# A two-layer hybrid decoder block: gate by tanh, gate projected ahead of the values, shared masks, one scaling product, two gain rows moved

## The chip, the cores and the metric

The kernel runs on one core of a Trainium2 chip. A core has five engines that run at the same time, each with its own instruction queue: TensorE (PE, matrix products; its weight loads are shown as PEld), VectorE (DVE), ScalarE (ACT), GpSimd (POOL) and SyncE (SP, which here only issues DMAs). The metric is the device time of one execution in microseconds, the median over several runs.

## The reference, cut to what matters

Two layers over 512 tokens of width 1024, in fp32. Each layer computes, from `h = x * (1 + sc1) + sh1`, one input projection whose columns feed three mixers:

- a gated MLP over chunks of 128 tokens (gMLP): GELU, a norm over 64 columns, a causal product over tokens;
- retention, 4 heads of 64: queries and keys are rotated, scores within a chunk are weighted by a decay mask, a state runs from chunk to chunk; the output is normed over each head and multiplied by `silu(g)`, where g is its own projection (`rg` in the kernel; q, k and v are `rq`, `rk`, `rv`);
- sparse attention, 8 heads on 2 key groups, with three branches, each weighted by a sigmoid gate per head and token: over compressed keys, over selected blocks, over a window. Here 512 tokens hold exactly the 8 blocks of 64 that are selected, and the window spans 512 tokens, so both of these are full causal attention, each with its own keys and values.

Then an output projection, `x = layer_norm(ALPHA * x + g1 * y)`, a gated feed-forward part with a causal convolution of width 3, and a second `layer_norm`. The shifts, scales and gates (adaLN) are products of the condition vector with `w_ada`.

## The kernel before, in words

Tokens are cut into 4 blocks of 128 (index t, i or c). Every fp32 product is made of three products of rounded parts (`mm3`, L445 to L447; `tm`, L538 to L540): each weight tile of 512 KB is loaded by SyncE's queue, rounded by ScalarE (L125) and its rest formed by VectorE or, for the retention and output weights, by GpSimd (L127). `Weights` holds the tiles as one list of jobs in the order of use, loaded up to three ahead.

The order on each engine is not quite that of the program text. A planner simulates the kernel and lets each engine take the earliest instruction of the program that is ready in the simulation; `tc.keep_in_program_order` pins an instruction behind the one traced before it on its engine.

One layer runs like this. (1) Projections of query and compressed keys; the gMLP's two halves U and Vv (`za0`, `za1`, GELU at L735); the compression's small products. (2) `cmp_scores` (L691), the values with the gates' columns (`vg`), then the norm of Vv (`norm64`, L464 to L475), the softmax over the compressed scores (transposes L702, softmax L707 to L718), the key projections `k`, the transposes of the softmax (L727) and the gMLP product (L808). (3) The attention's units: a unit is a head pair hp, a branch b (selected or window) and a block i. `scores` (L953 to L968) makes two products per head, adds the causal mask as a product of a bf16 identity with the mask (L955), takes the maximum, exponentiates on ScalarE (L964) and scales by reciprocal sum and gate (L968). Block 0 of both branches goes through `scores0` at once (L979 to L991). `transposes` (L999, L1000) and `pv_mm` (L1007, L1014) follow; scores are made two units ahead. Between the units `filler` runs one step of `retention` at a time: the four projections (`tm_all`, 8 steps each), then the chunks (L890 to L929), then the norm and the gate's product (L935). In layer 0 the steps also take adaLN products (L324). (4) Output projection, norms, feed-forward part.

X holds the residual. The last norm of layer 0 leaves its rows without gain; `last_gains(t)` multiplies X[t] by `lgr` and adds `lbr` in layer 1 (`gains`, L1143 and L1144, each 128x1024), rows 0 and 1 behind `za0`, rows 2 and 3 behind `cmp_scores`. `lgr`, `lbr`, U, Vv, the rotated queries and keys, the values `vb` and the gate `gb` share five buffers of the tag `m4`.

Of the kernel before, what the change touches and what calls it, by code (L numbers as in the profile page):

```python
# [13 lines left out]
AF = mybir.ActivationFunctionType  # L14
OP = mybir.AluOpType
AX = mybir.AxisListType

P = 128
S = 512
D = 1024  # L20
NT = S // P
# [12 lines left out]
C_ZA, C_QB, C_KB, C_VB, C_GB = 0, 512, 768, 1024, 1280  # L34
# [114 lines left out]
def tile_trunk(ctx, tc, I, tab, out, layers=L):  # L149
    nc = tc.nc  # L150
    V, A, G, T = nc.vector, nc.scalar, nc.gpsimd, nc.tensor
# [80 lines left out]
    for l in range(layers):  # L232
        if l == 0:
            for k in range(KD):
                rowk = I["w_in"][0][k * P:(k + 1) * P, :]
                jobs.append((("s", k), 768, [(lambda t: t[:, :768], rowk[:, C_QC:C_QC + 768])]))
        else:
            job_cols(("kc", l), l, [(C_KCM, P)])
            job_cols(("vc", l), l, [(C_VCM, P)])
            for r in range(4):  # L240
                job_cols(("q", l, r), l, [(C_QC + HD * (r + 4 * a), HD) for a in range(2)])
        job_tm(("za0", l), l, [(C_ZA, 256)])
        job_tm(("za1", l), l, [(C_ZA + 256, 256)])
        for k0, k1 in VGK:
            job_cols(("vg", l, k0), l, [(C_VSL, 128), (C_VWN, 152)], k0, k1)
        for b, c0 in enumerate((C_KSL, C_KWN)):
            job_cols(("k", l, b), l, [(c0, P)])
        aj = [j for bank in (1, 2) for j in ada_jobs(l, bank)] if l == 0 else []
        for n in range(32):
            if n % 8 in (0, 2):  # L250
                nm, c0 = (("rq", C_QB), ("rk", C_KB), ("rv", C_VB), ("rg", C_GB))[n // 8]
                h = n % 8 // 2
                job_cols((nm, l, h), l, [(c0, 256)], 4 * h, 4 * h + 4)
            if n in ADA_AT and aj:
                j = aj.pop(0)
                if j:
                    jobs.append(j)
        jobs.extend(j for j in aj if j)
        for cc, h in WO_ORDER:
            job_rows(("wo", l, cc, h), I["w_out"][l], 512 * h, 256, cc * 256, 4)  # L260
        wu = I["w_up"][l]
        for ct in range(NFF):
            for b in range(2):
                job_rows(("up", l, ct, b), wu, 0, P, b * DFF + ct * P, KD)
        for kk in range(NFF):
            job_rows(("dn", l, kk), I["w_down"][l], kk * P, D, 0, 1)
# [245 lines left out]
    for l in range(layers):  # L512
# [252 lines left out]
        next(za1)  # L765
        cmp_scores(kc)
        run(za1)
        if l:
            for t in range(2, NT):
                last_gains(t)  # L770


        VS = h4("vs", F32).rearrange("p b (t n) -> p b t n", t=NT)
        gates = pool.tile([P, NT, 24], F32, tag="gates", name="gates", bufs=1)
# [64 lines left out]
        def retention():  # L839
# [24 lines left out]
            for j, nm in enumerate(("rq", "rk")):  # L864
                def put(tp, pz, j=j):
                    for s in range(2):
                        rotate(pz[:, s * 256:(s + 1) * 256], R[j][:, 2 * tp + s, :], 2 * tp + s,
                               zx[:, 4 * j:4 * j + 4])
                yield from tm_all((nm, l), put)
            vb, gb = m4("vb"), m4("gb")  # L870
            yield from tm_all(("rv", l), lambda tp, pz: A.copy(vb[:, tp * 512:(tp + 1) * 512], pz))

            def put_g(tp, pz):
                d = gb[:, tp * 512:(tp + 1) * 512]
                A.activation(d, pz, AF.Exp, scale=-1.0)
                V.tensor_scalar(d, d, 1.0, None, op0=OP.add)
                V.reciprocal(d, d)
                V.tensor_tensor(d, d, pz, op=OP.mult)
            yield from tm_all(("rg", l), put_g)
            yield "projected"  # L880
            o = R[0].rearrange("p c n -> p (c n)")
            st = pool.tile([P, 4, HD], F32, tag="state", name="state", bufs=1)
# [49 lines left out]
            for hf in range(2):  # L932
                hs = slice(hf * 512, (hf + 1) * 512)
                norm64(o[:, hs], bl[:, 0, :], bl[:, 1, :], V)
                V.tensor_tensor(gb[:, hs], gb[:, hs], o[:, hs], op=OP.mult)  # L935
                yield
            RB["yb"] = gb

# [3 lines left out]
        def scores(hp, b, i):  # L942

            g = hp // 2
            n = P * (i + 1)
            if i == 1:
                bank = ps()
                o = [bank[:, e * 256:e * 256 + n] for e in range(2)]
            else:
                o = [ps()[:, :n] for e in range(2)]  # L950
            for e in range(2):
                qs = Q[g][:, 2 * (hp % 2) + e, i * P:(i + 1) * P]
                T.matmul(o[e], qs, KH[:, 2 * b + g, :n], start=True, stop=False)  # L953
                T.matmul(o[e], qs, KL[:, 2 * b + g, :n], start=False, stop=False)  # L954
                T.matmul(o[e][:, i * P:n], identb, cmaskb, start=False, stop=True)  # L955
            sm = pool.tile([P, 4, 2], F32, tag="sm", name="sm", bufs=4)
            if i == 1:
                V.reduce_max(sm[:, 0, :], bank.rearrange("p (e n) -> p e n", e=2)[:, :, :n], axis=AX.X, negate=True)
            else:
                for e in range(2):  # L960
                    V.reduce_max(sm[:, 0, e:e + 1], o[e], axis=AX.X, negate=True)  # L961
            pp = [pt(), pt()]
            for e in range(2):
                A.activation(pp[e][:, :n], o[e], AF.Exp, bias=sm[:, 0, e:e + 1], accum_out=sm[:, 1, e:e + 1])  # L964
            V.reciprocal(sm[:, 2, :], sm[:, 1, :])
            for e in range(2):
                c = 3 * (2 * hp + e) + 1 + b
                V.tensor_scalar(pp[e][:, :n], pp[e][:, :n], sm[:, 2, e:e + 1], gates[:, i, c:c + 1],  # L968
                                op0=OP.mult, op1=OP.mult)
            return pp  # L970

        def scores0(hp):
# [3 lines left out]
            for e in range(2):  # L976
                o = bank[:, e * 256:(e + 1) * 256].rearrange("p (b n) -> p b n", b=2)
                qs = Q[g][:, 2 * (hp % 2) + e, :P]
                T.matmul(o, qs, KH[:, g::2, :P], start=True, stop=False)  # L979
                T.matmul(o, qs, KL[:, g::2, :P], start=False, stop=False)  # L980
                T.matmul(o, identb, cmaskb[:, None, :].to_broadcast([P, 2, P]), start=False, stop=True)
            sm = pool.tile([P, 4, 2], F32, tag="sm", name="sm", bufs=4).rearrange("p (a c) b -> p a (c b)", a=2)
            b4 = bank.rearrange("p (j n) -> p j n", j=4)
            V.reduce_max(sm[:, 0, :], b4, axis=AX.X, negate=True)
# [1 line left out]
            for j in range(4):  # L986
                A.activation(pp[:, j, :], b4[:, j, :], AF.Exp, bias=sm[:, 0, j:j + 1], accum_out=sm[:, 1, j:j + 1])
            V.reciprocal(sm[:, 1, :], sm[:, 1, :])
            for j in range(4):
                c = 3 * (2 * hp + j // 2) + 1 + j % 2  # L990
                V.tensor_scalar(pp[:, j, :], pp[:, j, :], sm[:, 1, j:j + 1], gates[:, 0, c:c + 1],  # L991
                                op0=OP.mult, op1=OP.mult)
            return [[pp[:, 2 * e + b, :] for e in range(2)] for b in range(2)]

        def transposes(i, pp, PT):
# [354 lines left out]
        if l + 1 < layers:  # L1350
# [3 lines left out]
            def last_gains(t, gains=gains, lgr=lgr, lbr=lbr):  # L1354
                gains(t, lgr, lbr)
# [28 lines left out]
```

## Time and profile before

| | |
|---|---|
| runs | 1421.72 us median of 3 (1421.44 to 1424.19) |
| profiled execution | 1420.79 us, its span 1419.0 us |
| mean granted TensorE clock | 0.989 of full speed |
| ScalarE busy | 548.6 us (39%) |
| GpSimd busy | 216.1 us (15%) |
| HBM | 163.44 MB read, 2.10 MB written |

Times in the profile are microseconds from the first instruction. L12 is line 12 of the kernel. A row of a timeline gives the start, the duration, the engine, the line, the operation, the tiles out<-in with their shape, how many instructions are merged in the row, and in brackets how long the engine stood idle before it and on what it waited. Layer 0 takes the span up to about 750 us, layer 1 the rest; the attention with retention stands at about 130 to 305 us in layer 0 and 845 to 990 us in layer 1.

### The profile page before, as it was taken

How to read it: one execution, taken by the hardware profiler on the slowest of the kernel's cores; microseconds unless marked ns; L12 is line 12 of the kernel's file. 1: busy time of each engine (PE TensorE's matmuls, PEld its weight loads, DVE VectorE, ACT ScalarE, POOL GpSimd, SP SyncE). 2: the span in 40 equal slices, each digit the busy share in tenths (PEclk: the TensorE clock that was granted, in tenths of full speed). 3: DMA queues.
4: the chain of work that ended last, by engine and by line, in shares of the span. 5: the costliest groups of instructions: out<-in, count | busy, mean ns of one | idle time of the engine just before them, and what ended most of it. 6: DMA issues, size and time to landing. Idle time of an engine off the chain costs nothing.

```text
span 1419.0 us, 19802 instructions
## 1 busy us (share of the span) xinstructions
PE 1360.1 (96%) x7794; PEld 1117.2 (79%) x7794; DVE 887.7 (63%) x1463; ACT 548.6 (39%) x999; POOL 216.1 (15%) x212
## 2 busy tenths in 40 slices
PE   6999999999899999999999989999999999999995
PEld 4898665679887888778879978866898888888884
DVE  6668446656899566843466677486565555764337
ACT  2435333553343343332414245456254334343220
POOL 0311220335212010000020023111500000000005
PEclk9999999999999999999999999999999999999998
DMA  9832555512999353423424231110323333332221
GB/s 278 220 92 74 163 163 155 159 45 79 299 292 287 104 171 111 145 90 103 135 45 111 58 97 46 46 46 30 90 76 89 90 103 119 104 119 99 94 75 59
DMA packets 188012, 168.91 MB, mean 119 GB/s; under 512 B 23526, under 2 KB 167758, under 8 KB 187920
## 3 DMA queue, kind: packets, MB, share of 16 engines
q1 hardware_dynamic: 180368, 141.18, 34.1%
q0 software_dynamic: 7552, 26.48, 5.6%
q8 instruction: 61, 1.00, 0.3%
q14 instruction: 31, 0.25, 0.1%
HBM read 163.44 MB, written 2.10 MB: 117 GB/s over the span
## 4 chain that ended last, share of the span: by engine, by line
PE 85%; DVE 7%; issue 2%; DMA 2%; POOL 1%; SPq 1%; ACT 1%; DVEq 0%; POOLq 0%; ACTq 0%
PE ps L445 19%; PE ps L447 19%; PE ps L446 19%; PE ps L538 4%; PE ps L539 4%; PE ps L540 4%; PE ps L1007 3%; PE ps L324 2%; PE ps L999 2%; PE ps L953 1%; PE ps L954 1%; SPq L184 1%; DMA wraw<-in_w_up_dram 1%; POOL xa L1150 1%; PE ps L431 1%
## 5 line engine op out<-in xcount | busy, mean ns | idle before, releaser
L125 ACT CAST whi<-wraw 128x1024 fp32r<-128x1024 f32 (+4 forms) x188 | 186.6, 997 | 381.4 <-PE ps L446 199.0
L127 DVE TENSOR_TENSOR wlo<-wraw,whi 128x1024 fp32r<-128x1024 f32 (+3 forms) x162 | 187.2, 1158 | 181.1 <-ACT whi L125 180.8
L447 PE MATMUL ps<-h2h,wlo 128*128 128x512 f32 (+1 forms) x736 | 279.0, 379 | 0.0
L446 PE MATMUL ps<-h2l,whi 128*128 128x512 f32 (+1 forms) x736 | 277.7, 377 | 0.0
L445 PE MATMUL ps<-h2h,whi 128*128 128x512 f32 (+1 forms) x736 | 277.4, 378 | 0.0
L445 PEld LDWEIGHTS ps<-h2h,whi 128*128 128x128 f32 x736 | 138.8, 189 | 28.4 <-ACT whi L125 2.5
L446 PEld LDWEIGHTS ps<-h2l,whi 128*128 128x128 f32 x736 | 138.9, 189 | 27.2
L447 PEld LDWEIGHTS ps<-h2h,wlo 128*128 128x128 f32 x736 | 139.1, 189 | 26.1 <-issue 0.8
L538 PE MATMUL ps<-whi,hh 128*128 128x256 f32 (+1 forms) x448 | 131.9, 294 | 0.0
L539 PE MATMUL ps<-wlo,hh 128*128 128x256 f32 (+1 forms) x448 | 128.2, 286 | 0.0
L540 PE MATMUL ps<-whi,hl 128*128 128x256 f32 (+1 forms) x448 | 127.6, 285 | 0.0
L1150 POOL TENSOR_TENSOR xa<-xa,t 128x256 f32<-128x256 f32 (+1 forms) x30 | 35.8, 1200 | 525.7 <-DVE t L1149 525.7
L445 PE MATMUL ps<-whi,pt 128*128 128x512 f32 x288 | 113.9, 396 | 0.0
L446 PE MATMUL ps<-wlo,pt 128*128 128x512 f32 x288 | 113.9, 395 | 0.0
L447 PE MATMUL ps<-whi,pt 128*128 128x512 f32 x288 | 111.8, 396 | 0.0
L538 PEld LDWEIGHTS ps<-whi,hh 128*128 128x128 f32 x448 | 85.5, 191 | 14.8 <-issue 12.1
L539 PEld LDWEIGHTS ps<-wlo,hh 128*128 128x128 f32 x448 | 85.5, 191 | 4.5 <-issue 4.3
L540 PEld LDWEIGHTS ps<-whi,hl 128*128 128x128 f32 x448 | 85.4, 191 | 0.3 <-issue 0.3
L127 POOL TENSOR_TENSOR wlo<-wraw,whi 128x1024 fp32r<-128x1024 f32 x26 | 62.6, 2410 | 146.1 <-ACT whi L125 146.1
L187 DVE TENSOR_TENSOR pt<-g,pt 128x512 fp32r<-128x512 f32 x32 | 22.1, 691 | 81.9 <-PE ps L446 76.9
L1000 ACT COPY pT<-ps 128x128 f32<-128x128 f32 (+3 forms) x128 | 50.1, 438 | 55.3 <-PE ps L999 54.8
L964 ACT ACTIVATE pt<-ps,sm 128x256 f32<-128x256 f32 (+2 forms) x96 | 55.8, 590 | 37.9 <-DVE sm L961 26.9
(272 smaller groups left out, 2663.9 us busy)
## 6 DMA issues: line engine op xcount, KB each, us to landing
wraw<-in_w_up_dram SPq DMA_DIRECT2D x88, 512.0 KB, 4.0
araw<-in_w_ada_dram POOLq DMA_DIRECT2D x48, 512.0 KB, 5.4
wraw<-in_w_down_dram SPq DMA_DIRECT2D x44, 512.0 KB, 3.4
wraw<-in_w_ada_dram SPq DMA_DIRECT2D x32, 512.0 KB, 3.5
wraw<-in_w_in_dram SPq DMA_DIRECT2D x30, 512.0 KB, 3.8
wraw<-in_w_out_dram SPq DMA_DIRECT2D x16, 512.0 KB, 3.4
a<-in_w_ada_dram SPq DMA_DIRECT2D x14, 512.0 KB, 7.3
wraw<-in_w_in_dram SPq DMA_DIRECT2D x8, 384.0 KB
```

The source lines that it names most:

```text
L125: self.nc.scalar.copy(f(hi), src)
L127: eng.tensor_tensor(f(lo), src, f(hi).bitcast(F32), op=OP.subtract)
L445: T.matmul(o, lh, rh, start=first, stop=False)
L446: T.matmul(o, lh, rl, start=False, stop=False)
L447: T.matmul(o, ll, rh, start=False, stop=last)
L538: T.matmul(o, a, wh[:, k - k0, :], start=(first and k == 0), stop=False)
L539: T.matmul(o, a, wl[:, k - k0, :], start=False, stop=False)
L540: T.matmul(o, b, wh[:, k - k0, :], start=False, stop=(last and k == KD - 1))
L964: A.activation(pp[e][:, :n], o[e], AF.Exp, bias=sm[:, 0, e:e + 1], accum_out=sm[:, 1, e:e + 1])
L1000: A.copy(PT[e][:, i:i + 3 * i + 1:3, :], pb[:, :(i + 1) * P].rearrange("p (j q) -> p j q", q=P))
L1007: T.matmul(po[64 * e:64 * e + 64, j * P:], VS[:, b, j, 64 * g:64 * g + 64], PT[e][:, 4 * j:4 * j + NT - j, :].rearrange("p a q -> p (a q)" ...
L1150: eng.tensor_tensor(X[t][:, c0:c0 + n], X[t][:, c0:c0 + n], tmp, op=OP.add)
```

## The change

Five edits. In layer 1 the gain rows 2 and 3 are no longer scaled behind `cmp_scores` but behind the rotations of the first token pair of the query (row 2) and of the key (row 3). The gate's projection comes ahead of the values', in the job list too. The gate is formed as `(tanh(g/2) + 1) * g`, and the missing factor 0.5 is put into the last product, which becomes one of two operations. In `scores` with i = 1, where both heads share a PSUM bank, and in `scores0`, one mask product covers both heads, and only the bank's first product starts it. In `scores0` the four scalings (reciprocal sum times gate, per branch and head) become a small product of reciprocals and gates and one product over the whole tile.

```diff
-                nm, c0 = (("rq", C_QB), ("rk", C_KB), ("rv", C_VB), ("rg", C_GB))[n // 8]
+                nm, c0 = (("rq", C_QB), ("rk", C_KB), ("rg", C_GB), ("rv", C_VB))[n // 8]
...
         run(za1)
-        if l:
-            for t in range(2, NT):
-                last_gains(t)
...
                         rotate(pz[:, s * 256:(s + 1) * 256], R[j][:, 2 * tp + s, :], 2 * tp + s,
                                zx[:, 4 * j:4 * j + 4])
+                    if l and not tp:
+                        last_gains(2 + j)
                 yield from tm_all((nm, l), put)
             vb, gb = m4("vb"), m4("gb")
-            yield from tm_all(("rv", l), lambda tp, pz: A.copy(vb[:, tp * 512:(tp + 1) * 512], pz))
             def put_g(tp, pz):
                 d = gb[:, tp * 512:(tp + 1) * 512]
-                A.activation(d, pz, AF.Exp, scale=-1.0)
-                V.tensor_scalar(d, d, 1.0, None, op0=OP.add)
-                V.reciprocal(d, d)
-                V.tensor_tensor(d, d, pz, op=OP.mult)
+                A.activation(d, pz, AF.Tanh, scale=0.5)
+                V.scalar_tensor_tensor(d, d, 1.0, pz, op0=OP.add, op1=OP.mult)
             yield from tm_all(("rg", l), put_g)
+            yield from tm_all(("rv", l), lambda tp, pz: A.copy(vb[:, tp * 512:(tp + 1) * 512], pz))
...
-                V.tensor_tensor(gb[:, hs], gb[:, hs], o[:, hs], op=OP.mult)
+                V.scalar_tensor_tensor(gb[:, hs], gb[:, hs], 0.5, o[:, hs], op0=OP.mult, op1=OP.mult)
... scores(hp, b, i)
-                T.matmul(o[e], qs, KH[:, 2 * b + g, :n], start=True, stop=False)
+                T.matmul(o[e], qs, KH[:, 2 * b + g, :n], start=(not e or i > 1), stop=False)
                 T.matmul(o[e], qs, KL[:, 2 * b + g, :n], start=False, stop=False)
-                T.matmul(o[e][:, i * P:n], identb, cmaskb, start=False, stop=True)
+            if i == 1:
+                T.matmul(bank.rearrange("p (e n) -> p e n", e=2)[:, :, P:n], identb,
+                         cmaskb[:, None, :].to_broadcast([P, 2, P]), start=False, stop=True)
+            else:
+                for e in range(2):
+                    T.matmul(o[e][:, i * P:n], identb, cmaskb, start=False, stop=True)
... scores0(hp)
-                T.matmul(o, qs, KH[:, g::2, :P], start=True, stop=False)
+                T.matmul(o, qs, KH[:, g::2, :P], start=not e, stop=False)
                 T.matmul(o, qs, KL[:, g::2, :P], start=False, stop=False)
-                T.matmul(o, identb, cmaskb[:, None, :].to_broadcast([P, 2, P]), start=False, stop=True)
+            T.matmul(bank.rearrange("p (j n) -> p j n", j=4), identb, cmaskb[:, None, :].to_broadcast([P, 4, P]),
+                     start=False, stop=True)
...
-            for j in range(4):
-                c = 3 * (2 * hp + j // 2) + 1 + j % 2
-                V.tensor_scalar(pp[:, j, :], pp[:, j, :], sm[:, 1, j:j + 1], gates[:, 0, c:c + 1],
-                                op0=OP.mult, op1=OP.mult)
+            V.tensor_tensor(sm[:, 1, :].rearrange("p (e b) -> p e b", e=2), sm[:, 1, :].rearrange("p (e b) -> p e b", e=2),
+                            gates[:, 0, 6 * hp:6 * hp + 6].rearrange("p (e k) -> p e k", k=3)[:, :, 1:3], op=OP.mult)
+            V.tensor_tensor(pp, pp, sm[:, 1, :, None].to_broadcast([P, 4, P]), op=OP.mult)
```

## Rows read from the trace of the kernel before

**Rows 1.** The page's first part: busy us (share of the span) xinstructions.
```profile
PE 1360.1 (96%) x7794; PEld 1117.2 (79%) x7794; DVE 887.7 (63%) x1463; ACT 548.6 (39%) x999; POOL 216.1 (15%) x212
```

**Rows 2.** TensorE's waits: line <- releaser: us in total, times, longest us.
```profile
PE ps L727 <- DVE pt L718: 5.4, 2, 5.2
...
PE ps L324 <- DMA wraw<-in_w_ada_dram: 2.0, 1, 2.0
```

**Rows 3.** Two stretches: length, busy us by engine, then granted clock, DMA share, GB/s.
```profile
833.00:838.00 5.00, 5.00 (x17) 4.23 (x17) 3.59 (x6) 1.81 (x4) 0.00 (x0) 0.51 0.39 108
...
254.00:258.00 4.00, 4.00 (x25) 1.91 (x24) 1.86 (x7) 0.00 (x0) 0.00 (x0) 0.57 0.50 169
```

**Rows 4.** Timeline of TensorE in layer 0, early stage.
```profile
112.84 1.04 PE L702 MATMUL ps<-tb,cs 128*128 128x128 f32 x8
...
119.54 0.63 PE L727 MATMUL ps<-tb,pt 128*128 128x128 f32 x4 [0.20 <-DVE pt L718]
...
126.34 1.89 PE L808 MATMUL ps<-Vv,t 128*128 128x256 f32 x8
```

**Rows 5.** Timeline of TensorE in layer 1, same stage.
```profile
821.08 1.04 PE L702 MATMUL ps<-tb,cs 128*128 128x128 f32 x8
...
832.77 1.08 PE L727 MATMUL ps<-tb,pt 128*128 128x128 f32 x4 [5.18 <-DVE pt L718]
...
842.04 1.89 PE L808 MATMUL ps<-Vv,t 128*128 128x256 f32 x8
```

**Rows 6.** Timeline of VectorE in layer 1, same stage.
```profile
807.82 1.22 DVE L1143 TENSOR_TENSOR xa<-xa,lg 128x1024 f32<-128x1024 f32 x1
...
813.57 0.17 DVE L465 TENSOR_SCALAR nst<-nst 128x8 f32<-128x8 f32 x1
813.65 1.22 DVE L1144 TENSOR_TENSOR xa<-xa,lb 128x1024 f32<-128x1024 f32 x1
...
829.15 0.16 DVE L712 TENSOR_TENSOR csm<-csm,gates 128x16 f32<-128x16 f32 x1
...
829.98 2.31 DVE L712 TENSOR_TENSOR csm<-csm,gates 128x16 f32<-128x16 f32 x1
```

**Rows 7.** Timeline of VectorE in layer 0, the second half's norm.
```profile
103.08 0.17 DVE L465 TENSOR_SCALAR nst<-nst 128x8 f32<-128x8 f32 x1
```

**Rows 8.** VectorE's groups by line and shape: busy us, mean ns | idle before.
```profile
L877 DVE RECIPROCAL gb<-gb 128x512 f32<-128x512 f32 x4 | 13.4, 3348 | 0.1
...
L878 DVE TENSOR_TENSOR gb<-gb,ps 128x512 f32<-128x512 f32 x4 | 2.7, 673 | 0.0
```

**Rows 9.** Timeline of TensorE in layer 1, first retention chunks.
```profile
935.16 0.41 PE L916 MATMUL ps<-vb,t 128*128 128x64 f32 x2 [2.24 <-DVE t L904]
...
939.63 0.41 PE L916 MATMUL ps<-vb,t 128*128 128x64 f32 x2 [0.40 <-ACT pt L964]
```

**Rows 10.** Timeline of VectorE in layer 1, during the values' projection.
```profile
912.82 1.04 DVE L961 TENSOR_REDUCE sm<-ps 128x1 f32<-128x384 f32 x2 [7.67 <-PE ps L955]
```

**Rows 11.** Timeline of TensorE in layer 1: scores of block 0 and of block 1.
```profile
918.18 0.28 PE L980 MATMUL ps<-kl,q 128*128 128x256 f32 x1
...
918.54 0.28 PE L980 MATMUL ps<-kl,q 128*128 128x256 f32 x1
...
922.44 0.28 PE L954 MATMUL ps<-kl,q 128*128 128x256 f32 x1
...
922.80 0.28 PE L954 MATMUL ps<-kl,q 128*128 128x256 f32 x1
```

**Rows 12.** Timeline of VectorE in layer 1: block 0's four scalings.
```profile
960.61 1.10 DVE L991 TENSOR_SCALAR pt<-pt,sm,gates 128x128 f32<-128x128 f32 x4
```

**Rows 13.** ScalarE's groups: the table loads ahead of the gates.
```profile
L782 ACT ACT_TABLE_LOAD x2 | 2.6, 1283 | 0.0
```

**Rows 14.** Timeline of VectorE in layer 1, behind the query and the key rotations.
```profile
861.40 0.69 DVE L958 TENSOR_REDUCE sm<-ps 128x2 f32<-128x512 f32 x1 [2.35 <-PE ps L955]
...
879.59 0.18 DVE L988 RECIPROCAL sm<-sm 128x4 f32<-128x4 f32 x1 [1.43 <-ACT pt L987]
```

## The prediction

> **What bounds the kernel now.** I read the share of busy time first: TensorE is busy 96% of the span, VectorE 63% [rows 1]. So a saving on VectorE counts only where TensorE waits for it, and a saving on TensorE counts almost everywhere. The next view is therefore TensorE's own waits. The reader is to see there one wait of 5.2 us for the compression softmax (L727 for L718) and, in layer 0, one of 2.0 us for a weight transfer [rows 2]. The third view is the granted clock by stretches: behind each of the two waits the clock stands at its lower level, 1.2 of 2.4 GHz, for a while. From 833 to 838 us the mean is 0.51, which loses 5.0 x (1 - 0.51) = 2.45 us; from 254 to 258 it is 0.57, which loses 4.0 x 0.43 = 1.7 us [rows 3].
>
> The 5.2 us wait has a control inside the same trace, because layer 0 runs the same stage without the four gain instructions. From the transposes of the compression scores (L702) to the first gMLP product (L808) layer 0 takes 126.34 - 112.84 = 13.50 us and its wait at L727 is 0.20 us [rows 4]. Layer 1 takes 842.04 - 821.08 = 20.96 us with a wait of 5.18 [rows 5]. The difference is 7.46 us; the wait (5.18 - 0.20 = 4.98) and the lower clock (2.45) make 7.43 of it.
>
> **Part 1: two gain rows leave layer 1's early stage.** The four instructions of L1143 and L1144 at 807.82 to 813.65 take 1.22 us each, 4.9 us of VectorE [rows 6]. The second half's first scaling in the gMLP norm (L465) starts 7.51 us before L702 in layer 1 (813.57) and 9.76 us before it in layer 0 (103.08) [rows 6, 7]: the chain is 2.25 us late by then, with the last gain still to come. What is late runs into GpSimd's weight splits: the tiny L712 takes 0.16 us alone and 2.31 us the second time [rows 6]. Without the four instructions layer 1 has layer 0's instruction list here, so I take layer 0's stage: 7.4 us off. Bounds: if one such collision of 2.3 us stays on the path and the clock falls all the same, 7.4 - 2.3 - 2.45 = 2.6 us are left; if the wait goes entirely, 5.18 + 2.45 = 7.6.
>
> **Part 2: where these gain rows go.** They are pinned behind the rotations of the first token pair of the query and of the key projection; the X rows that they scale are needed only by the output projection's residual, over 100 us later. Queued behind each pair of them (2.4 us) are the reductions and scalings of the attention's softmax, for which TensorE's transposes (L999) wait. VectorE stands idle 2.35 us just before 861.40, behind the query rotations, and 1.43 us just before 879.59, behind the key rotations [rows 14]. 2.44 - 2.35 leaves 0.1 and 2.44 - 1.43 leaves 1.0, and the second has projection products in front of its transposes. I take +0.3 us; ends 0 and 1.1, or, with no cover at all, 4.9. The multiplier rows lgr and lbr also hold two of the five 4 KB buffers longer, until the key rotation; the gate and the values, which need two, are written only after that.
>
> **Part 3: the gate.** Each half gate now is an exponential, an addition, a reciprocal (3.35 us) and a product from PSUM (0.67 us) [rows 8]. After it is a tanh and one two-operation product, which I price as the old product. VectorE loses at least 3.35 us per half, 13.4 in all. In layer 0 TensorE has the adaLN products there and does not wait for it, so nothing is counted. In layer 1 the reciprocals stand before the decay mask of the first retention chunks (L904), and TensorE waits 2.24 and 0.40 us for these at 935 and 940 [rows 9]: 2.6 us off. The move ahead of the values helps too: at the values' old place VectorE is idle 7.67 us in one piece [rows 10], and what is copied last (the values) is ScalarE's. Bounds 0 (another VectorE instruction is late next, as in the dense tail of the attention) and 2.8. The other way round, the first chunk's product with the values now follows their copy by one step of the interleaving instead of two projections; the copy is one ScalarE instruction, the first token pair's is done a half projection earlier, so I count nothing, at worst 0.6 us a layer. The two projections' weight loads swap places in the same queue, with equal sizes.
>
> **Part 4: masks of both heads in one product.** In block 1 the second low-order product starts at 922.44, the next head's at 922.80: 0.36 us for the product itself, a mask and one more product; in block 0, with a mask of 256 columns, 918.18 to 918.54 are 0.36 too [rows 11]. With 0.12 us for each of the other two, a mask costs 0.12 us whether it has 128 or 256 columns. Block 1 drops one of two masks in 16 units (4 head pairs, 2 branches, 2 layers): 16 x 0.12 = 1.9 us on the bound engine. In block 0 two masks of 256 columns become one of 512, for which there is no row; it costs between one and two masks, so the saving is between 0 and 8 x 0.12 = 1.0. I take 0, nearer to the columns. Ends of the part: 1.0 (layer 0's half swallowed by its weight transfers) and 2.9.
>
> **Part 5: block 0 scaled in one product.** Four scalings take 1.10 us [rows 12]; a small product (0.16, row L712 [rows 6]) and one of 512 columns (0.67, L878 [rows 8]) take 0.83. 0.27 us less, 8 times. Only the last head pair of each layer stands in a tail where TensorE waits for VectorE, so 0.5 us in all; ends 0 and 2.2. The Trainium skill (VectorE: DVE Perf Modes, section "Mode 2×_2P") says that a scaling by scalars in fp32 passes two elements a cycle and a product of two tensors only one, which speaks against this edit. By its rate alone (0.96 GHz) four times 128 columns are 0.27 us and 512 columns 0.53, an estimate that makes the edit 0.27 us slower each time, 2.1 in all; the rows show that the fixed part of four instructions outweighs this. The half factor in the last gate product replaces one instruction by one: nothing.
>
> **The sum.** 7.4 + 2.6 + 1.9 + 0.5 - 0.3 = 12.1 us. The profiled execution took 1420.79 us (span 1419.0), so 1408.7 by its own time; it lies 0.93 us below the median of the runs, 1421.72, and on that scale the forecast is **1409.6 us**.
>
> **The rivals.** (a) The wait moves instead of going: the gain rows hold up the softmax at the rotations for their full 4.9 us, and a lower clock follows as at 833 (2.45), so that part 1 is undone. 1409.6 + 4.9 + 2.45 - 0.3 = 1416.7 us. For it: VectorE is the late engine in that stretch at times; against: the two idle pieces of rows 14. 8 in 100. (b) The change does not do what it says because the order is laid out anew by a planner: the same instructions are left out, but another instruction meets GpSimd's splits in the early stage. Only part 1's lower end: 1409.6 + 4.8 = 1414.4. 10 in 100. (c) Slower than before: tanh lies in another table than exp. The trace has a table load of 1.28 us where ScalarE changes function [rows 13] and no tanh at all. Four gate halves would each cost two loads (to tanh, back to exp) between softmax exponentials; TensorE, which gets its transposes' inputs from there, waits 2.57 us each time and loses clock as after the 2.0 us wait at 253 (1.7 us [rows 2, 3]): 4 x (2.57 + 1.7) = 17.1, that is 1426.7 us. It decides from a full load pair uncovered in at least three of four halves. Against it: VectorE's and ScalarE's other functions (copy, square, identity) cause no load. 4 in 100. The Trainium skill (ScalarE: Activation LUTs, section "Table sets: the hidden batching unit") lists tanh in the table of exp; by that rule there is no further load, and no run here shows it yet.
>
> **How the numbers follow.** The forecast has 74 in 100, with its own range 1405 to 1413; (a) to (c) have 22; 4 are left for a new wait that the new order makes anywhere. Downward, layer 0's wait for weights (2.0 + 1.7) may vanish and block 0's masks gain 1.0: 1409.6 - 4.7 = 1404.9. Upward, (b) and, nearly, (a): 1416. Range 1404.5 to 1416. A measurement tells changes over 0.2%, 2.8 us, so faster means under 1418.9: the forecast, (a), (b) and a part of the rest, 0.91; same 0.04; slower 0.05.
>
> **What would show it.** Right: the wait at L727 in layer 1 under 1 us, the clock at 2.4 GHz all through that stage, 13.5 to 14.5 us from L702 to L808; no wait over 0.5 us at L916; 80 masks of the later blocks where there were 96 and 8 of block 0 where there were 16; seven table loads as before. Wrong: a wait of 2 us or more at L999 behind the gain rows, a table load beside a tanh, or a saving under 6 us though the wait at L727 is gone.

## The result, and the profile after

The changed kernel takes 1410.57 us (median of 4 runs, 1409.93 to 1411.42); the kernel before, on the same chip, 1421.58 us (4 runs). The ratio is 0.9927 [0.9914, 0.9939], 11.0 us less. The forecast was 1409.6 us, 12.1 less, with a range of 1404.5 to 1416. The total came out as forecast; two of its terms did not, and they happen to cancel. The profiled execution took 1411.42 us (span 1409.6), the longest of the four.

In this part of the document lines are those of the changed kernel where nothing else is said: L808 became L804, L916 L912, L968 L969, L999 L1000, L1160 L1161. In an experiment the edit can shift a line by a few more.

First the page: busy us (share of the span) x instructions, after.

```profile
PE 1357.1 (96%) x7770; PEld 1119.5 (79%) x7770; DVE 868.5 (62%) x1439; ACT 548.6 (39%) x999; POOL 217.4 (15%) x212
```

Against [rows 1] TensorE has 24 instructions fewer (the masks) and VectorE 19.2 us less work. As before, that second number says little: what counts is where TensorE waited. One of its waits before, then those after (line, releaser: us in total, times, longest):

```profile
PE ps L999 <- DVE pt L968: 2.8, 6, 0.8
```

```profile
PE ps L431 <- DVE xa L1161: 12.2, 4, 5.1
...
PE ps L1000 <- DVE pt L969: 5.8, 5, 1.9
...
PE ps L727 <- DVE pt L718: 0.4, 2, 0.2
```

The long wait at L727 of [rows 2] is gone. In its place the attention's transposes (L1000) now wait 5.8 us for the softmax scalings, where they waited 2.8 before. TensorE's timeline in layer 1's early stage, and the stage's stretches (length, busy us by engine, then granted clock, DMA share, GB/s):

```profile
819.84 1.04 PE L702 MATMUL ps<-tb,cs 128*128 128x128 f32 x8
...
826.55 0.63 PE L727 MATMUL ps<-tb,pt 128*128 128x128 f32 x4 [0.21 <-DVE pt L718]
...
833.37 1.89 PE L804 MATMUL ps<-Vv,t 128*128 128x256 f32 x8
```

```profile
820.00:830.00 10.00, 9.79 (x53) 8.05 (x51) 8.55 (x18) 6.00 (x15) 4.82 (x2) 1.00 0.47 133
830.00:840.00 10.00, 10.00 (x63) 8.64 (x62) 5.88 (x11) 4.95 (x9) 2.37 (x1) 1.00 0.37 105
```

From L702 to the first gMLP product it is 833.37 - 819.84 = 13.53 us, against 20.96 [rows 5] and layer 0's 13.50 [rows 4]; the clock stays at its upper level, 2.4 GHz. That is part 1, to a tenth of a microsecond. Some 20 us later comes what the prediction missed. TensorE after, in the rotations of the query:

```profile
853.92 0.63 PE L1000 MATMUL ps<-tb,pt 128*128 128x128 f32 x4 [0.96 <-DVE pt L969]
...
856.40 0.63 PE L1000 MATMUL ps<-tb,pt 128*128 128x128 f32 x4 [1.86 <-DVE pt L969]
```

VectorE, after, over the same time, and GpSimd (start, us, then the instruction):

```profile
847.76 1.22 DVE L1144 TENSOR_TENSOR xa<-xa,lg 128x1024 f32<-128x1024 f32 x1
...
850.06 1.20 DVE L1145 TENSOR_TENSOR xa<-xa,lb 128x1024 f32<-128x1024 f32 x1
851.18 2.59 DVE L969 TENSOR_SCALAR pt<-pt,sm,gates 128x512 f32<-128x512 f32 x1
...
853.69 2.57 DVE L969 TENSOR_SCALAR pt<-pt,sm,gates 128x512 f32<-128x512 f32 x1
```

```profile
850.03 3.46 POOL L127 TENSOR_TENSOR wlo<-wraw,whi 128x1024 fp32r<-128x1024 f32 x1 [0.58 <-ACT whi L125]
...
853.44 2.53 POOL L127 TENSOR_TENSOR wlo<-wraw,whi 128x1024 fp32r<-128x1024 f32 x1
```

The first gain row to be moved (row 2) is taken at 847.76 to 851.26. Two scalings of 128x512 (L969) stand behind it and so start at 851.18, into two weight splits of GpSimd. The splits end at 853.49 and 855.97, the scalings at 853.77 and 856.26: they end 0.28 and 0.29 us behind a split, and take 2.6 us each. In the kernel before the same two scalings were under way when the first split came, and the second split came only at 864.85; VectorE and GpSimd there:

```profile
858.05 1.00 DVE L968 TENSOR_SCALAR pt<-pt,sm,gates 128x512 f32<-128x512 f32 x2
```

```profile
858.73 2.58 POOL L127 TENSOR_TENSOR wlo<-wraw,whi 128x1024 fp32r<-128x1024 f32 x1 [1.07 <-ACT whi L125]
```

That is 1.00 us for both. The Trainium skill (SBUF — State Buffer, section "Who interferes with whom") says that VectorE and GpSimd have one pair of memory ports in common, and that whichever starts first keeps it for its whole instruction while the other is blocked. The trace agrees for the scalings: they start into the splits and end with them. It also shows the other side, since the split of 850.03 took 3.46 us instead of 2.53 beside a gain instruction that ran in its usual 1.20; by the profile the split started 0.03 us before that instruction, too little to say which was first. e7, below, has a clear case.

Behind gain row 3 VectorE meets a split too, and TensorE does not wait. VectorE, after, behind the key's first rotations:

```profile
877.27 2.36 DVE L991 TENSOR_TENSOR sm<-sm,gates 128x4 f32<-128x4 f32 x1
```

This small product takes 0.15 us elsewhere. TensorE runs projection products meanwhile and shows no wait between 858 and 920 us, so it isn't the collision by itself that costs; at the query's two waits no projection product stands between 851.4 and 860.4.

Behind the two waits the clock falls, as it did at 833 in the kernel before [rows 3]. Stretch of after, columns as above:

```profile
857.00:860.50 3.50, 3.50 (x10) 1.58 (x9) 2.76 (x11) 1.60 (x5) 1.23 (x2) 0.51 0.54 150
```

3.5 x (1 - 0.51) = 1.7 us. The two profiled executions can now be set against each other, place by place (us):

| place | before | after | difference |
|---|---|---|---|
| layer 1, L702 to the first gMLP product | 20.96 | 13.53 | -7.4 |
| query rotations: waits, lower clock | 0.23, none | 2.82, 1.7 | +4.3 |
| first retention chunks: waits | 2.64 | none | -2.6 |
| 16 masks of 0.12; scaling (as priced) | | | -1.9; -0.5 |
| layer 0, wait for weights with its lower clock | 3.7 | none | -3.7 |
| layer 0, first norm, last block (L431), wait and lower clock | 3.9, 1.7 | 5.1, 2.8 | +2.3 |
| 27 to 35 us, lower clock | 1.7 | 3.4 | +1.7 |
| sum | | | -7.8 |
| span | 1419.0 | 1409.6 | -9.4 |

"First norm" is the one behind the output projection; L431 transposes its rows, and the last of the four token blocks is the one that waits. The 1.6 us that are left lie in small pieces that I did not follow. Three rows of the table aren't in the prediction's sum: the weights (an end of its range), the norm, and the start. The start's rows, before and then after:

```profile
27.00:35.00 8.00, 7.69 (x32) 6.27 (x32) 7.09 (x17) 3.19 (x6) 0.00 (x0) 0.79 1.17 310
```

```profile
27.00:35.00 8.00, 7.57 (x24) 6.43 (x25) 7.19 (x18) 3.21 (x6) 0.00 (x0) 0.57 1.16 311
```

Busy times and transfers are the same to a few per cent; the clock differs. Whether that belongs to the change is a question for a repeat of it (e10, below).

Last, what the edits issue. Groups by shape, after: busy us, mean ns of one, idle time before.

```profile
L873 DVE SCALAR_TENSOR_TENSOR gb<-gb,ps 128x512 f32<-128x512 f32 x4 | 2.7, 683 | 4.2 <-ACT gb L872 4.2
...
L993 DVE TENSOR_TENSOR pt<-pt,sm 128x512 f32<-128x512 f32 x8 | 5.5, 690 | 0.1
...
L956 PE MATMUL ps<-cmaskb,identb 128*128 128x128 bf16 x64 | 10.6, 227 | 0.0
L952 PE MATMUL ps<-cmaskb,identb 128*128 128x256 bf16 x16 | 4.5, 283 | 0.0
L982 PE MATMUL ps<-cmaskb,identb 128*128 128x512 bf16 x8 | 3.1, 390 | 0.0
...
L735 ACT ACT_TABLE_LOAD x2 | 2.6, 1283 | 0.0
L778 ACT ACT_TABLE_LOAD x2 | 2.6, 1283 | 0.0
L1254 ACT ACT_TABLE_LOAD x2 | 2.6, 1283 | 1.4 <-DVE t L1252 1.4
```

The gate's one product takes 683 ns where the old product took 673 [rows 8], and the reciprocals are gone. There are 80 masks of the later blocks and 8 of block 0, as foretold, and TensorE's longest wait at L912 is 0.2 us. The table loads are those of [rows 13] with the same two further lines and one at the start, seven as before, and none beside the tanh: rival (c) is settled. The Trainium skill (ScalarE: Activation LUTs, section "Table sets: the hidden batching unit") puts tanh into exp's table, and the trace now agrees.

### The profile page after: what moved, and what is told of

It is laid out like the page before. It is cut to its first block, busy times and chain, and to the rows that moved or that the text cites. A ratio compares the mean times of both kernels' runs of the same rounds, so it can differ in the third digit from the quotient of the medians.

```text
span 1409.6 us, 19729 instructions
## 1 busy us (share of the span) xinstructions
PE 1357.1 (96%) x7770; PEld 1119.5 (79%) x7770; DVE 868.5 (62%) x1439; ACT 548.6 (39%) x999; POOL 217.4 (15%) x212
## 4 chain that ended last, share of the span: by engine, by line
PE 86%; DVE 5%; DMA 2%; ACT 2%; SPq 1%; issue 1%; POOL 1%; DVEq 0%; ACTq 0%; POOLq 0%
PE ps L445 20%; PE ps L447 20%; PE ps L446 20%; PE ps L538 4%; PE ps L539 4%; PE ps L1008 4%; PE ps L540 4%; PE ps L324 2%; PE ps L1000 2%; PE ps L949 1%; PE ps L950 1%; SPq L184 1%; DMA wraw<-in_w_up_dram 1%; PE ps L431 1%; POOL xa L1151 1%
## 5 line engine op out<-in xcount | busy, mean ns | idle before, releaser
L538 PEld LDWEIGHTS ps<-whi,hh 128*128 128x128 f32 x448 | 85.5, 191 | 14.8 <-issue 12.1
L1250 ACT ACTIVATE t<-ps,pcol 128x512 f32<-128x512 f32 x88 | 68.1, 774 | 1.7 <-PE ps L447 1.7
```

What stands on the lines that cost most here:

```text
L538: T.matmul(o, a, wh[:, k - k0, :], start=(first and k == 0), stop=False)
L1250: A.activation(a, pa, AF.Identity, bias=cwc[:, 3, cx:cx + 1], scale=cwc[:, 2, cx:cx + 1])
```

## The experiments

Ratios are to the kernel before, with 95% intervals, from 5 to 12 runs each. For differences the changed kernel's 0.9927 is the mark; 0.001 is 1.4 us. The runs of one group (e1 to e4, e5 to e8, e9 to e11) were made on the same chip; for these groups the kernel before has 1420.85, 1420.47 and 1421.96 us.

**e1: the gain rows back in the early stage.** This undoes parts 1 and 2 and keeps the rest.

```diff
         run(za1)
+        if l:
+            for t in range(2, NT):
+                last_gains(t)
...
-                    if l and not tp:
-                        last_gains(2 + j)
```

> The changed kernel, with gain rows 2 and 3 back behind the compression scores. Theory A (read from the two traces): the move won 7.4 us in layer 1's early stage (wait at L727 5.0, lower clock 2.45) and paid 4.3 us at the query rotations (waits at L1000 of 0.96 and 1.86 less 0.2, and 3.4 us at the lower clock, 1.7). So the time rises by 3.1 us, to about 1413.6, and the wait of some 5 us at L727 is back. Theory B (the prediction's term): the new place costs 0.3 us, so the time rises by 7.1 us, to about 1417.6.

1413.29 us, 0.9945 [0.9932, 0.9958]: 2.6 us above the changed kernel by the ratios, 2.7 by the medians, not the 7.1 that parts 1 and 2 were to give. Yet the wait is back in full. TensorE in e1, and the stretch behind it:

```profile
832.24 1.09 PE L727 MATMUL ps<-tb,pt 128*128 128x128 f32 x4 [5.19 <-DVE pt L718]
```

```profile
829.00:837.00 8.00, 4.76 (x17) 4.17 (x18) 7.06 (x9) 2.75 (x6) 2.73 (x1) 0.57 0.41 124
```

From L702 to the first gMLP product e1 takes 20.46 us, 6.9 more than the changed kernel. So part 1 has nearly its size, and something gives back 4.2 to 4.3 us of it: 6.9 less the 2.6 to 2.7 that remain, against the 4.3 read from the waits at 853 to 856. The 7.1 that the prediction's terms give would be a ratio of 0.9977, outside the interval.

**e2: both gain rows behind the key's rotations.** Row 2 leaves the query's stage, row 3 stays where it was.

```diff
-                    if l and not tp:
-                        last_gains(2 + j)
+                    if l and j:
+                        last_gains(2 + tp)
```

> The changed kernel, with both gain rows behind the key rotations (row 2 behind the first token pair, row 3 behind the second) and none behind the query rotations. Theory A: the waits at L1000 behind the query rotations (2.6 us more than before the change) and the lower clock after them (1.7) go, and nothing takes their place, since VectorE has idle pieces there: about 4.3 us less, 1406.3. Theory B: these waits have another cause (the new order of the scores), and the time stays at 1410.6 within 1 us.

1405.5 us, 0.9902 [0.9887, 0.9916]. That is the lowest median of all kernels here: 5.1 us below the changed one by medians, 3.6 by the ratios; the two intervals touch, so the order of the two is likely rather than sure. The place is plain, though. VectorE, then GpSimd, in e2:

```profile
851.28 1.00 DVE L969 TENSOR_SCALAR pt<-pt,sm,gates 128x512 f32<-128x512 f32 x2
...
871.37 1.22 DVE L1144 TENSOR_TENSOR xa<-xa,lg 128x1024 f32<-128x1024 f32 x1
```

```profile
852.20 2.38 POOL L127 TENSOR_TENSOR wlo<-wraw,whi 128x1024 fp32r<-128x1024 f32 x1 [1.32 <-ACT whi L125]
...
858.01 2.40 POOL L127 TENSOR_TENSOR wlo<-wraw,whi 128x1024 fp32r<-128x1024 f32 x1 [3.44 <-ACT whi L125]
```

The scalings are again 1.00 us, done as the split starts, and the clock (third column from the end) is at its upper level throughout:

```profile
840.00:870.00 30.00, 29.68 (x224) 26.17 (x224) 23.11 (x67) 14.81 (x47) 7.41 (x6) 1.00 0.18 52
870.00:900.00 30.00, 30.00 (x232) 26.51 (x231) 22.76 (x45) 16.14 (x43) 14.11 (x8) 1.00 0.17 54
```

The gain rows thus can stand behind the key's rotations at no visible cost; it is row 2 behind the query's that cost. The rows show a second thing that row 2 did there. In e2 the second split starts 5.81 us behind the first, in the changed kernel 3.41 us, since ScalarE rounds that tile ahead of the copies of the transposes and in e2 behind them. The gain row made the scalings about 2 us late, and the order that came with it also brought the second split 2.4 us earlier, into the second scaling.

**e3 and e5: the gate's two edits, undone one at a time.** e3 keeps the gate ahead of the values, with the old chain; e5 keeps the tanh, at the old place.

```diff
 e3
-                A.activation(d, pz, AF.Tanh, scale=0.5)
-                V.scalar_tensor_tensor(d, d, 1.0, pz, op0=OP.add, op1=OP.mult)
+                A.activation(d, pz, AF.Exp, scale=-1.0)
+                V.tensor_scalar(d, d, 1.0, None, op0=OP.add)
+                V.reciprocal(d, d)
+                V.tensor_tensor(d, d, pz, op=OP.mult)
 e5
-            yield from tm_all(("rg", l), put_g)
             yield from tm_all(("rv", l), lambda tp, pz: ...)
+            yield from tm_all(("rg", l), put_g)
```

> The changed kernel, with the gate by exponential, addition, reciprocal and product again, its projection still ahead of the values. Theory A: what the gate's part won is the reciprocals leaving the stretch of the first chunks, and the earlier place alone does that already, because VectorE idles there: the time rises by less than 1 us, to at most 1411.5. Theory B (the prediction): the 2.6 us of waits come back, about 1413.2. In both the waits at L912 tell: none over 0.5 us in A, 2 us in B.

> The changed kernel, with the values projected ahead of the gate again; the gate stays a tanh. Theory A: the two edits of the gate cover each other, since either of them alone takes the reciprocals out of the first chunks' way (the run with the exponential gate at the new place rose by 0.75 us only): here too less than 1 us, at most 1411.6, and no wait over 0.5 us at the product of scores and values (L916 of the kernel before). Theory B: the order itself is worth the 3 to 4 us that the other runs leave over between the kernel before and the changed one with the gain rows back: about 1414.

e3: 1411.32 us, 0.9934 [0.9922, 0.9946]. e5: 1410.53 us, 0.9926 [0.9911, 0.9942]. Neither differs from the changed kernel by more than its interval. Read singly, the gate's part is worth nothing, which is what a theory "VectorE's work there was hidden" says too. Only undoing both at once tells these apart.

**e9: both gate edits undone together** (the two diffs above in one kernel).

> The changed kernel, with both edits of the gate undone: exponential gate, and the values projected first. Theory A (the two edits cover each other): one alone undone cost 0.75 us and 0.0 us, both together bring back the 2.2 and 0.4 us of waits in layer 1's first chunks and, if the clock falls after them, up to 1.7 us: 2.6 to 4.3 us more, 1413.2 to 1414.9. Theory B (additive): 0.75 us more, 1411.3.

1415.38 us, 0.9962 [0.9947, 0.9976], against 1409.95 of the changed kernel on the same chip (e10): 5.4 us. The edits cover for each other: with the gate early the reciprocal is done in time, and with tanh there is no reciprocal to be late. TensorE in e9, then VectorE, then the stretch behind:

```profile
929.40 0.33 PE L1002 MATMUL ps<-tb,pt 128*128 128x128 f32 x1 [1.28 <-ACT pt L967]
...
930.60 0.43 PE L914 MATMUL ps<-vb,t 128*128 128x64 f32 x2 [0.87 <-DVE t L902]
```

```profile
924.83 3.34 DVE L875 RECIPROCAL gb<-gb 128x512 f32<-128x512 f32 x1
```

```profile
932.00:935.00 3.00, 3.00 (x17) 2.77 (x16) 2.81 (x6) 0.89 (x2) 0.00 (x0) 0.53 0.00 0
```

The waits are 1.28 + 0.87 = 2.15 us, in the size of [rows 9], the first of them by way of ScalarE, and behind them 3.0 x 0.47 = 1.4 us go to the lower clock. In layer 1, from the first L727 to the first transposes of the norm behind the output projection (L431), e9 takes 190.85 us and e10 186.37: 4.5 us, of which these rows give 3.6.

**e4 and e11: the masks**, each head its own again in the changed kernel (e4), and shared masks alone in the kernel before (e11). The diff is e4's; e11 has it the other way round.

```diff
-                T.matmul(o[e], qs, KH[:, 2 * b + g, :n], start=(not e or i > 1), stop=False)
+                T.matmul(o[e], qs, KH[:, 2 * b + g, :n], start=True, stop=False)
                 T.matmul(o[e], qs, KL[:, 2 * b + g, :n], start=False, stop=False)
+                T.matmul(o[e][:, i * P:n], identb, cmaskb, start=False, stop=True)
-            if i == 1:
-                T.matmul(bank.rearrange("p (e n) -> p e n", e=2)[:, :, P:n], identb,
-                         cmaskb[:, None, :].to_broadcast([P, 2, P]), start=False, stop=True)
...
-                T.matmul(o, qs, KH[:, g::2, :P], start=not e, stop=False)
+                T.matmul(o, qs, KH[:, g::2, :P], start=True, stop=False)
                 T.matmul(o, qs, KL[:, g::2, :P], start=False, stop=False)
-            T.matmul(bank.rearrange("p (j n) -> p j n", j=4), identb, cmaskb[:, None, :].to_broadcast([P, 4, P]),
-                     start=False, stop=True)
+                T.matmul(o, identb, cmaskb[:, None, :].to_broadcast([P, 2, P]), start=False, stop=True)
```

> The changed kernel, with one mask product for each head again. Theory A: 16 masks of 0.12 us come back on the bound engine and nothing in block 0: 1.9 us, about 1412.5; the bound with block 0 is 2.9. Theory B: the new order that followed the merged masks also removed layer 0's wait for a weight transfer (2.0 us and 1.7 us of clock), so that comes back with them: 5.6 us, about 1416. Theory C: hidden under other limits, within 0.7 us of 1410.6.

> The kernel before, with nothing but the shared mask products. Theory A: 16 masks of 0.12 us on the bound engine: 1.9 us less than before, about 1418.6, with 2.9 as the bound. Theory B: less, under 1 us, because layer 0's half stands beside the adaLN weight transfers and layer 1's tail waits for the softmax.

e4: 1412.81 us (1408.86 to 1417.69), 0.9943 [0.9925, 0.996], 2.2 us above the changed kernel, with a wide interval. e11: 1420.88 us, 0.9995 [0.9986, 1.0005], 1.1 us under its kernel before, which this measurement can't tell from nothing. Both leave room for the 1.9 us of part 4, and neither shows it. Nor do the two profiles differ from their partners by the masks alone. In e4 the wait at the query's rotations is one of 3.79 us, where the changed kernel has 0.96 and 1.86. In e11 the wait of [rows 9], 2.24 us before, is longer by 1.36:

```profile
933.30 0.41 PE L915 MATMUL ps<-vb,t 128*128 128x64 f32 x2 [3.60 <-DVE t L903]
```

Another place that may stand against the gain is layer 0's first norm, at its last token block. TensorE there, before, then after:

```profile
365.76 1.09 PE L431 MATMUL ps<-tb,xa 128*128 128x128 f32 x8 [3.94 <-DVE xa L1160]
```

```profile
363.40 1.97 PE L431 MATMUL ps<-tb,xa 128*128 128x128 f32 x8 [5.13 <-DVE xa L1161]
```

This wait is 3.94 us in the kernel before, 3.96 in e4 and 3.82 in e7, which have separate masks; 5.13, 5.04 and 5.00 in the changed kernel, e10 and e11, and 5.00 to 5.67 in the seven other runs, which all share them. It goes with an accumulation of weights on VectorE just ahead of that norm, which in the changed kernel stands idle for a transfer:

```profile
356.12 1.28 DVE L342 SCALAR_TENSOR_TENSOR acc<-araw,ce,acc 128x1024 f32<-128x1024 f32 x1 [1.01 <-DMA araw<-in_w_ada_dram]
```

A layer 0 that arrives earlier at a transfer which doesn't would look like this, but e4 speaks against it: its wait begins at 356.66 us, before the changed kernel's 358.27, and VectorE has no such idle time ahead of that norm. So the longer wait goes with the shared masks in every run, and how they bring it about is open.

**e6: four scalings in block 0 again.**

```diff
-            V.tensor_tensor(sm[:, 1, :] ..., gates[:, 0, 6 * hp:6 * hp + 6] ..., op=OP.mult)
-            V.tensor_tensor(pp, pp, sm[:, 1, :, None].to_broadcast([P, 4, P]), op=OP.mult)
+            for j in range(4):
+                c = 3 * (2 * hp + j // 2) + 1 + j % 2
+                V.tensor_scalar(pp[:, j, :], pp[:, j, :], sm[:, 1, j:j + 1], gates[:, 0, c:c + 1],
+                                op0=OP.mult, op1=OP.mult)
```

> The changed kernel, with four scalings of 128 columns in block 0 again. Theory A (the prediction): 0.5 us more, 1411.1, with ends 1410.6 and 1412.8. Theory B: four short instructions also meet GpSimd's weight splits (3.17 and 3.23 us where they take 1.1 alone), as the single product does too, so there is no difference beyond 0.5 us. Theory C (the slower rate of a product of two tensors): 1 to 2 us less, about 1409.

1411.15 us, 0.9928 [0.9912, 0.9943]. That is 0.6 us more by medians, 0.1 by ratios: nothing that can be told from none.

**e7: the gains' move alone, in the kernel before** (e1's diff, the other way round).

> The kernel before, with nothing but the gain rows moved to the query and key rotations. Theory A: the win at L727 (7.4 us) less the wait and the lower clock behind the query rotations (4.3), as in the changed kernel: 3 us less than before, about 1418. Theory B: the edits help each other, and alone the move is worth nothing or the whole 7.4: within 0.5 us of before, or under 1414.

1419.44 us, 0.9993 [0.9981, 1.0004]: 1.0 us less, where 3 were expected. TensorE in e7, two waits and the stretch behind each:

```profile
855.61 1.17 PE L997 MATMUL ps<-tb,pt 128*128 128x128 f32 x8 [3.15 <-DVE pt L966]
...
931.05 0.41 PE L914 MATMUL ps<-vb,t 128*128 128x64 f32 x2 [2.24 <-DVE t L902]
```

```profile
856.00:861.00 5.00, 4.84 (x20) 2.43 (x19) 3.96 (x16) 2.46 (x7) 1.37 (x2) 0.66 0.36 105
...
931.00:936.00 5.00, 4.95 (x28) 4.07 (x30) 4.06 (x12) 1.75 (x7) 0.00 (x0) 0.66 0.00 0
```

The stage of part 1 takes 13.51 us here too. The wait at the query's rotations takes 3.15 + 5.0 x 0.34 = 4.9 us of part 1's 7.4. In e7 it is the gain instruction that meets the first split, and the split is clearly first, by 0.27 us; VectorE, then GpSimd:

```profile
849.73 3.34 DVE L1142 TENSOR_TENSOR xa<-xa,lb 128x1024 f32<-128x1024 f32 x1
```

```profile
849.46 2.53 POOL L127 TENSOR_TENSOR wlo<-wraw,whi 128x1024 fp32r<-128x1024 f32 x1 [0.34 <-ACT whi L125]
```

The gain instruction takes 3.34 us instead of 1.22 and ends 1.08 us behind the split, and the split is not held up. The second wait is the kernel before's own, 2.24 us in both [rows 9], but here 1.7 us of lower clock follow it, as they did not in the profiled execution of before: -7.4 + 4.9 + 1.7 = -0.8, near the 1.0 measured.

**e8: the key projection's weight splits on VectorE instead of GpSimd**, to take the collision away without moving a gain row.

```diff
-on_pool = ("rq", "rk", "rv", "rg", "wo")
+on_pool = ("rq", "rv", "rg", "wo")
```

> The changed kernel, with the rests of the two key weights formed by VectorE instead of GpSimd (1.23 us each). Theory A: what costs behind the query gain row is that the block-3 scalings (L969) start 2.3 us later and so meet GpSimd's splits of these weights (5.08 us for two, which take 1.0 alone); without these splits VectorE wins more than the 2.5 us it takes on: the waits at L1000 behind the query rotations fall from 2.8 us in sum to under 1.5, and the time falls by 1 to 4 us. Theory B: the cost is the 2.3 us of VectorE's time alone; 2.5 us more of it there makes the waits longer, 4 us or more in sum, and the time rises by 1 to 3 us.

1411.38 us, 0.9934 [0.9914, 0.9953]. VectorE at the disputed place in e8, then TensorE somewhat earlier:

```profile
852.15 1.00 DVE L969 TENSOR_SCALAR pt<-pt,sm,gates 128x512 f32<-128x512 f32 x2
```

```profile
846.10 0.49 PE L1000 MATMUL ps<-tb,pt 128*128 128x128 f32 x2 [3.06 <-DVE pt L993]
```

Without GpSimd's splits the scalings take 1.00 us although gain row 2 ends only 1 us ahead of them (849.98 + 1.21), so it is the collision, and not the 2.4 us of the row, that made them 5 us. The time is no lower, since block 0's scaling (L993) is late instead and TensorE waits 3.06 us for it: in the new order the rotations' products stand ahead of that scaling on VectorE, where the changed kernel has them behind it.

**e10: the changed kernel once more**, unedited, to see what differs between executions of one kernel.

> The changed kernel once more, for what differs from one execution to another. Theory A: layer 0's wait for an adaLN weight transfer (2.0 us before, under 0.3 in the first profile of the changed kernel) and the number of low-clock stretches near 38 and 373 us come and go between executions of one program, so this profile shows some of them otherwise than the first, within a median of 1409.5 to 1411.5. Theory B: they belong to the order of the changed kernel and stand as in its first profile.

1409.95 us (1408.3 to 1413.26), 0.9922 [0.9908, 0.9935]. Two stretches of e10:

```profile
27.00:35.00 8.00, 7.44 (x31) 6.13 (x32) 7.33 (x18) 3.45 (x6) 0.00 (x0) 0.79 1.16 309
...
262.00:266.00 4.00, 4.00 (x15) 2.19 (x14) 3.84 (x7) 1.22 (x3) 4.00 (x5) 0.57 0.67 202
```

The start's clock is that of the kernel before, 0.79, and there is a lower clock at 262 that the first execution lacks. So 1.7 us at the start come and go with the execution. The waits at 853 to 856 (5.8 us over all at L1000) are the same in both, and so is the one at L431, though the lower clock behind it takes 1.9 us in e10 (0.68 over 363.99 to 370) and 2.8 in the first execution. Layer 0's wait for weights is absent in both, so e10 does not show it to come and go, as was expected; but it is 2.0 in the kernel before, none in e1, 1.55 in e2, 0.72 in e7 and 1.57 in e11, and e1 and e2 have the same text in layer 0 as the changed kernel. Its 3.7 us are therefore not counted as the change's, and their cause is open. What differs between executions is no part of the change.

## Why the prediction was right, and where it was not

**Part 1 (-7.4): right.** The stage takes 13.53 us, as in layer 0; e1 brings the wait of 5.19 back, and 6.9 of the 7.4 us. Reading the one layer as a control for the other gave the number.

**Part 2 (+0.3): the term that failed, at +4.3.** The prediction took 2.35 us of VectorE's idle time ahead of 861.40 [rows 14] as cover for gain row 2. That idle time lay behind the scalings in question, which ran at 858.05: the row was queued ahead of them, where there was no gap. And it priced the delay as a delay (2.44 us less the cover), not as what it meets: two scalings came to stand in two splits, and 1.00 us became 5.08. The bound without cover, 4.9, held the number by luck: it was reckoned as the delay of two rows, and what was paid is one row's collision and a lower clock. For row 3 no wait followed, though VectorE lost 2.2 us to the split at 877.27 alone, more than the 1.43 us of cover: TensorE had projection products to run there, which the prediction named beside the cover. The sign that was to prove the prediction wrong, a wait of 2 us or more at L1000 behind the gain rows, did not come: it was two waits of 0.96 and 1.86.

**Part 3 (-2.6): right in kind, likely too small; 4.5 (stage, e9 against e10) to 5.4 (medians).** The waits that go are the 2.2 to 2.6 read from [rows 9]. The lower clock that follows such a wait was counted for L727 and for the weights, but not here, since the profiled execution of before showed none. e7, e9 and e11 show it, with 1.4 to 1.7 us. That the move and the tanh are one remedy given twice was not foreseen: either alone suffices (e3, e5).

**Parts 4 and 5 (-1.9, -0.5): fit, not proven.** The runs give 2.2 and 1.1 us for the masks with intervals wide enough to hold 1.9, or nothing in e11, and 0.1 to 0.6 for the scaling. The prices of single instructions are right where they are seen: the scaling is 0.15 + 0.69 = 0.84 us against the 0.83 that was worked out. For the mask of 512 columns, taken as dear as two of 256, the row has 390 ns against 283, so it is under two; whether the path gained by it no run shows.

**The sum.** -7.4 + 4.3 - 4.5 (or 5.4) - 1.9 - 0.5 is -10.0 to -10.9, and 11.0 were measured. The forecast's 12.1 was near by luck: part 2 cost 4.0 us more than priced, part 3 gained 2 to 3 us more, and the two have opposite signs. The longer wait of the first norm in layer 0 stands in no term. Taken alone, two edits gave less than taken out of the whole, the gains 1.0 (e7) against 2.7 (e1) and the masks 1.1 (e11) against 2.2 (e4). In the profiles a wait further on takes up part of what is gained (the lower clock at 931 in e7, the longer wait at 933 in e11), but the intervals are too wide to call the difference shown.

**The rivals.** (a) came half true: the wait did move, to the query's rotations, with a lower clock behind it, but as 4.3 us, not 7.4, and through GpSimd's splits rather than through the rows' own length alone. (b) had the right partner for the collision and the wrong place. (c) is out: no table load.

## What to carry to other kernels

Before moving work into an idle gap of an engine, look at which side of the gap the instruction stands that others wait for: cover counts only if it lies between the moved work and that instruction. Then ask what the delayed instruction will run beside; on VectorE, whether GpSimd's long two-input operations start there, and whether TensorE has other products to run meanwhile. And price a wait of one engine as the wait plus the lower clock that has been seen behind its like, even where one trace doesn't show it; undo two edits that aim at the same wait together, because one at a time they show nothing.

## What the runs showed of the hardware

A scaling of 128x512 in fp32 takes 0.50 us on VectorE and 2.6 us when it meets one weight split on GpSimd, ending 0.3 us behind it. Of a gain instruction and a split that meet, the split took 3.46 us instead of 2.53 in the changed kernel, where the two start within 0.03 us, and the gain instruction 3.34 instead of 1.22 in e7, where the split starts 0.27 us earlier. A wait of about 2.2 us at the same place and line was followed by the lower of TensorE's two clock levels in e7 (0.66 over 5 us) and not in the profiled execution of the kernel before. And one kernel's first 35 us can differ by 1.7 us with the same work and the same transfers (0.57 and 0.79 of the clock over 8 us), which is more than parts 2 and 5 were priced at, and nearly part 4.
